# First projections of a two-layer attention backbone: products of constants ahead, a new loading order, scale and shift in one copy, context products one block late

## The chip, the cores and the metric

The kernel runs on one core of one Trainium2 chip. The metric is the device time of one execution in microseconds (us); less is better. TensorE (PE in the profile) multiplies matrices, VectorE (DVE), ScalarE (ACT) and GpSimd (POOL) work on elements, and SyncE's queue (SP) issues most DMA transfers.

## The reference, cut to what matters

Two layers over 512 latent and 256 context tokens of width 1024, all in float32. What the change touches is the head of the first layer:

```python
mod = c_silu @ ada_w + ada_b                      # for the latents; cctx_silu for the context
shift, scale, gate = jnp.split(mod, 3, axis=-1)
hx = rmsnorm(x, norm_w) * (1 + scale[:, None, :]) + shift[:, None, :]
hc = rmsnorm(cx, norm_w) * (1 + scale_c) + shift_c
px = split_cols(hx @ w_in)
pc = split_cols(hc @ w_in)
...                                               # three kinds of attention, gate, output projection
```

## The kernel before, in words

Activations lie transposed: features on the 128 partitions, tokens along the free axis. The width 1024 is 8 blocks of 128 features (`kt` 0 to 7). Set `s` = 0 is the 512 latents, `s` = 1 the 256 context tokens. Every float32 product is made from three faster ones: each operand is split into a rounded part (`hh` of the activations, `wh` of the weights) and the rest (`hl`, `wl`), and `wh*hh`, `wh*hl` and `wl*hh` are added up in PSUM.

The first stage (lines 384 to 461) makes, block by block, the normed and modulated activations, and with each block adds its part to three early projections: a query tile and a key tile of the neighbourhood attention (`WF_BQ`, `WF_BK`: 512 latent columns and 256 context columns each) and a value tile (`WT_BV`: six token tiles `t`, four of latents, two of context, 256 columns each). These sums stay open in PSUM over all eight blocks.

- `load_x(s)` (L392) loads the tokens, 8 DMAs of 256 KB for the latents and 8 of 128 KB for the context.
- `ada_load(k)` (L199) loads 1 MB of modulation weights for block k in two halves, from 9 buffers. `ada(k)` makes 8 float32 products with them (L214, 16 records in the profile), copies the result (L218), transposes it twice (L222), and gets scale and shift by small DVE operations (L225, L228, L231).
- `norm_x(s)` squares the 8 blocks on ACT (L351), adds them up on DVE (L355), sums over partitions by products with ones (L359), takes the power -0.5 (L366 on DVE, L369 on POOL), spreads the result over the partitions by transposes (L378), and copies it from PSUM to SBUF on ACT (L401).
- `make_h(kt, s)`: DVE multiplies x by scale and norm (L408), ACT adds the shift and rounds (L409, `hh`), and the rest `hl` comes from DVE in one operation (L411) where `kt % 2 == s`, and from POOL in two (L413, L414) otherwise.
- `load_w1` loads 512 columns of weights (L256, 3 buffers); `split` makes `wh` on ACT (L247) and `wl` on DVE or POOL (L250).
- `spread_silu` (L135, L138, L139) prepares rows that a much later stage uses.
- `bc`, loaded at L81, holds the q/k norm weights and the sink logits, the same on each partition; `negsink` (L89) is made from it. The first later user is L810.

The program is written with a scheduler that plays the instructions through a time model and gives each engine one fixed order; `high_priority` moves instructions ahead in it, and `after(a, b)` keeps a behind b in that order without a semaphore. The first stage ends in L430 products; then the remaining projections (L341, L318) and the attention of both layers follow.

Of the kernel before, what the change touches and what calls it, by code (L numbers as in the profile page):

```python
# [20 lines left out]
KT = 8  # L21
# [42 lines left out]
def body(tc, xT, small, bcast, rpb, adaw, adat, wt, wf, wo, trigA, trigC, mskB, mskC, outT):  # L64
# [16 lines left out]
    nc.sync.dma_start(bc, bass.AP(tensor=bcast.tensor, offset=bcast.offset, ap=[[0, 128], [1, BC_N]]))  # L81
# [7 lines left out]
    nc.vector.tensor_scalar(negsink, bc[:, BC_SINK:BC_SINK + 16], -1.0, None, op0=OP.mult)  # L89
# [105 lines left out]
    def ada_load(k, pool, tag, bufs):  # L195
        sts = []
        for half in range(2):
            st = pool.tile([128, 4, 256], F32, name="ada", tag=tag, bufs=bufs)
            nc.sync.dma_start(st, adaw[k, half])  # L199
            sts.append(st)  # L200
        return sts

    def ada(k, sts, bank):
# [5 lines left out]
        with ExitStack() as at_once:  # L209
            if k >= KT:  # L210
                at_once.enter_context(tc.high_priority(offset=2000))
            for n, half in enumerate(halves):
                for g in range(4):
                    nc.tensor.matmul(pm[32 * g:32 * g + 2, 0:256], silu_c[:, half * 4 + g, :],  # L214
                                             sts[half][:, g, :], start=(n == 0), stop=(n == 1), skip_group_check=True)
        sb = wpool.tile([128, 256], F32, name="adasb", bufs=1)
        if k < KT:
            nc.scalar.activation(sb, pm[:, 0:256], AF.Copy)  # L218
        else:
            nc.vector.tensor_copy(sb, pm[:, 0:256])  # L220
        for i in range(2):
            nc.tensor.transpose(pm[:, 256 + i * 128:384 + i * 128], sb[:, i * 128:(i + 1) * 128], ident)  # L222
        for i, (l, third, j) in enumerate(ADA[k]):
            m = modT[l, third][:, j, :]
            nc.vector.tensor_reduce(m, pm[:, 256 + i * 128:384 + i * 128].rearrange("p (g q) -> p q g", g=4)[:, 0:2, :],  # L225
                                    axis=AX.X, op=OP.add)
            if third == 1:
                nc.vector.tensor_scalar(m, m, abw[:, l, 0, j:j + 1], abw[:, l, 1, j:j + 1], op0=OP.mult, op1=OP.add)  # L228
            else:
                c = SM_AB + l * 24 + third * 8 + j  # L230
                nc.vector.tensor_scalar(m, m, sm[:, c:c + 1], None, op0=OP.add)  # L231

# [11 lines left out]
    def split(src, shape, room=None):  # L244

        hi, lo = room or [wpool.tile([128, 512], F32R, name=n) for n in ("wh", "wl")]
        nc.scalar.activation(hi, src, AF.Copy)  # L247
        wlo["n"] += 1
        eng = nc.vector if wlo["by"][wlo["n"] % len(wlo["by"])] == "D" else nc.gpsimd
        eng.tensor_sub(lo, src, hi.bitcast(F32))  # L250
# [3 lines left out]
    def load_w1(dram_ap, i, shape):  # L254
        st = wpool.tile([128, 512], F32, name="ws", bufs=CFG["ws"])
        pace["sp"] = nc.sync.dma_start(st, dram_ap[:, i * 512:(i + 1) * 512]).ins.name  # L256
        return split(st, shape)
# [126 lines left out]
    with tc.tile_pool(name="p0", bufs=1, reuse_waits="tile") as p0:  # L384
# [9 lines left out]

        def norm_x(s):
            n = SETS[s][1] - SETS[s][0]
            sums = []
            for kt in range(KT):
                add_sq(sums, xs[s, kt], kt, n, p0, lambda: Obig[:, s * 8:])
            r = p0.tile([128, n], F32, name=f"rb{s}")  # L400
            nc.scalar.activation(r, rstd_rows(sums[1], n, p0, Sbig[:, s * 512:s * 512 + n])[:, 0:n], AF.Copy)  # L401
            rb[s] = r

        def make_h(kt, s):
            A, B = [modT[0, t][:, kt, s:s + 1] for t in (1, 0)]
            n = SETS[s][1] - SETS[s][0]
            x = xs[s, kt]
            nc.vector.scalar_tensor_tensor(x, x, A, rb[s], op0=OP.mult, op1=OP.mult)  # L408
            nc.scalar.activation(hh[kt][s], x, AF.Identity, bias=B)  # L409
            if kt % 2 == s:  # L410
                nc.vector.scalar_tensor_tensor(hl[kt][s], x, B, hh[kt][s].bitcast(F32), op0=OP.add, op1=OP.subtract)  # L411
            else:
                nc.gpsimd.tensor_scalar(x, x, B, None, op0=OP.add)  # L413
                nc.gpsimd.tensor_sub(hl[kt][s], x, hh[kt][s].bitcast(F32))  # L414
# [3 lines left out]
        sts = {0: ada_load(0, p0, "ada", CFG["a0"])}  # L418
        load_x(1)
        norm_x(0)  # L420
        norm_x(1)
        early["f", WF_BQ] = [pj(), Obig[:, 0:256]]
# [4 lines left out]
        def part(key, out, a, b, kt, i):  # L427
# [5 lines left out]
            elif kt == 0:  # L433
                after(mm, opened[key].ins.name)

        for kt in range(KT):
            if kt < KT - 1:
                sts[kt + 1] = ada_load(kt + 1, p0, "ada", CFG["a0"])
            if kt % 4 == 0:
                wq = {s: load_w1(wf[0, s], kt // 4, (4, 128)) for s in (WF_BQ, WF_BK)}  # L440
            if kt % 2 == 0:
                wv = load_w1(wt[0, WT_BV, kt // 4], kt // 2 % 2, (2, 256))
            hh[kt], hl[kt] = new_h(), new_h()
            with tc.high_priority(offset=CFG["h1"]):
                ada(kt, sts.pop(kt), psT)
                for s in range(2):
                    make_h(kt, s)
                wrap_h(kt)
            for x, s in enumerate((WF_BQ, WF_BK)):
                wh, wl = wq[s]  # L450
                for g, (c0, n) in enumerate(((0, NT), (NT, NCX))):
                    for i, (a, b) in enumerate(((wh, hh), (wh, hl), (wl, hh))):
                        part(("c", 0) if g else ("l", x), early["f", s][g][:, 0:n], a[:, kt % 4, :], cols(b[kt], c0, n),
                             kt, i)
            wh, wl = wv
            for t in (1, 2, 3, 4, 5, 0):
                p = early["t", WT_BV][t // 2][:, t % 2 * 256:t % 2 * 256 + 256]
                for i, (a, b) in enumerate(((hh, wh), (hh, wl), (hl, wh))):
                    part(("v", t // 2), p, off_tile(a[kt], t), b[:, kt % 2, :], kt, i)
            if kt in (1, 2, 3, 4):  # L460
                spread_silu(kt - 1, p0)
# [1209 lines left out]
```

## Time and profile before

| | |
|---|---|
| median of 3 runs | 1198.84 us (1198.54 to 1199.2) |
| span of the profiled execution | 1197.7 us; the page lists no other time for it, and the runs stand 0.8 to 1.5 us above |
| PE busy | 1150.5 us, 96% |
| DVE / ACT / POOL busy | 769.4 / 696.9 / 408.1 us |
| granted TensorE clock, mean | 0.996 |
| first L430 product | 22.10 us after the span's start |
| last L430 product | starts at 68.80 us |

A row of the timeline gives start, duration, engine, line, operation, what is written from what, a count, and in brackets the idle time before and what ended it. A busy PE is not PE at its peak, since matmuls overlap: their pace is read from the distance of their starts. `PEld` is the loading of the stationary operand; `SPq` is an issue in SyncE's queue.

### The profile page before, as it was taken

The numbers are of one execution on the slowest core, as the hardware profiler recorded it, in microseconds if no ns is written. First come the engines' busy times: TensorE is split into PE (matmuls) and PEld (weight loads), VectorE is DVE, ScalarE is ACT, GpSimd is POOL, SyncE is SP. The second block draws the span as 40 slices with busy tenths as digits, with TensorE's granted clock in tenths as the row PEclk, the third lists the DMA queues.
The fourth block names the chain that finished last, engine by engine and source line by source line (L and its number), as shares of the span: only waits on it lengthen the run. The fifth ranks groups of instructions, "written<-read, shape, count | busy, mean of one in ns | idle before, by whom it ended". The sixth has DMA issues, their size and how long they took to land.

```text
span 1197.7 us, 21749 instructions
## 1 busy us (share of the span) xinstructions
PE 1150.5 (96%) x8016; PEld 1034.8 (86%) x8016; DVE 769.4 (64%) x1548; ACT 696.9 (58%) x1581; POOL 408.1 (34%) x496
## 2 busy tenths in 40 slices
PE   5999999999999999999999999999999999998997
PEld 3898999998898988988778999989988888887876
DVE  5767566764656665568578895567754556567563
ACT  5446555656666676588423544555666667677552
POOL 1341110234446354385000030202274563656001
PEclk9999999999999999999999999999999999999999
DMA  9552222313312112123086662323222111232152
GB/s 321 213 142 89 78 78 67 123 66 104 111 70 92 67 44 92 34 63 119 27 293 198 205 210 74 98 84 109 91 73 67 53 46 53 63 88 72 36 161 77
DMA packets 60826, 124.22 MB, mean 104 GB/s; under 512 B 7216, under 2 KB 13488, under 8 KB 60720
## 3 DMA queue, kind: packets, MB, share of 16 engines
q1 hardware_dynamic: 54768, 111.96, 29.6%
q10 hardware_dynamic: 5952, 10.88, 2.7%
q8 instruction: 63, 1.03, 0.3%
q14 instruction: 43, 0.35, 0.1%
HBM read 109.05 MB, written 11.14 MB: 100 GB/s over the span
## 4 chain that ended last, share of the span: by engine, by line
PE 81%; DVE 5%; ACT 5%; DMA 3%; issue 3%; POOL 1%; SPq 0%; ACTq 0%; DVEq 0%; POOLq 0%
PE pj L318 18%; PE pj L341 17%; PE Sbig L1049 9%; PE Obig L1049 9%; PE T L1054 9%; PE pj L519 5%; PE T L519 3%; PE Sbig L519 3%; PE T L341 2%; PE Sbig L430 2%; DVE ptl L1044 1%; DMA x<-xT_dram 1%; PE Sbig L341 1%; ACT pth L798 1%; PE pj L430 1%
## 5 line engine op out<-in xcount | busy, mean ns | idle before, releaser
L1044 DVE TENSOR_TENSOR ptl<-T,pth 128x512 fp32r<-128x512 f32 (+2 forms) x312 | 181.1, 591 | 128.6 <-ACT pth L798 126.7
L798 ACT ACTIVATE pth<-T 128x512 fp32r<-128x512 f32 (+2 forms) x312 | 158.9, 520 | 134.8 <-PE T L1054 128.1
L341 PE MATMUL pj<-wh,hL 128*128 128x256 f32 x896 | 180.6, 287 | 0.0
L318 PE MATMUL pj<-hL,wh 128*128 128x512 f32 x544 | 175.0, 401 | 0.9 <-ACT wh L247 0.5
L1054 PE MATMUL T<-ident,P 128*128 128x128 f32 x1024 | 165.7, 273 | 4.0 <-ACT qt L902 1.7
L247 ACT ACTIVATE wh<-ws 128x512 fp32r<-128x512 f32 x192 | 119.5, 629 | 78.6 <-PE pj L318 16.3
L1049 PE MATMUL Sbig<-kt,qt 128*128 128x256 f32 (+1 forms) x864 | 156.2, 308 | 4.6 <-ACT P L1160 2.5
L250 POOL TENSOR_TENSOR wl<-ws,wh 128x512 fp32r<-128x512 f32 x76 | 98.5, 1300 | 146.4 <-ACT wh L247 146.4
L341 PEld LDWEIGHTS pj<-wh,hL 128*128 128x128 f32 x896 | 144.2, 190 | 1.0 <-issue 0.2
L1049 PE MATMUL Obig<-pth,vt 128*128 128x256 f32 (+2 forms) x432 | 134.6, 321 | 4.6 <-ACT pth L798 2.0
L1054 PEld LDWEIGHTS T<-ident,P 128*128 128x128 f32 x1024 | 123.0, 140 | 17.6 <-DVE ptl L1044 2.2
L1049 PE MATMUL Obig<-ptl,vt 128*128 128x256 f32 (+2 forms) x432 | 131.4, 318 | 5.0 <-DVE ptl L1044 4.3
L1049 PEld LDWEIGHTS Sbig<-kt,qt 128*128 128x128 f32 x864 | 123.3, 189 | 13.4 <-DVE negm L1208 4.1
L341 PE MATMUL pj<-wl,hL 128*128 128x256 f32 x448 | 128.0, 286 | 0.0
L318 PEld LDWEIGHTS pj<-hL,wh 128*128 128x128 f32 x544 | 96.2, 189 | 16.7 <-ACT wh L247 0.9
L250 DVE TENSOR_TENSOR wl<-ws,wh 128x512 fp32r<-128x512 f32 x116 | 82.7, 720 | 40.4 <-ACT wh L247 31.6
L318 PE MATMUL pj<-hL,wl 128*128 128x512 f32 x272 | 107.1, 394 | 0.5 <-DVE wl L250 0.5
L1049 PEld LDWEIGHTS Obig<-pth,vt 128*128 128x128 f32 x432 | 81.6, 189 | 15.9 <-ACT pth L798 7.1
L1049 PEld LDWEIGHTS Obig<-ptl,vt 128*128 128x128 f32 x432 | 81.5, 189 | 14.7 <-DVE ptl L1044 11.3
L1445 POOL TENSOR_TENSOR bm<-wr,bm 128x192 f32<-128x192 f32 (+1 forms) x48 | 41.3, 888 | 139.6 <-DMA bm<-mskB_dram 132.4
L341 PEld LDWEIGHTS pj<-wl,hL 128*128 128x128 f32 x448 | 85.4, 191 | 0.3
L1158 DVE TENSOR_REDUCE negm<-Sbig 128x1 f32<-128x768 f32 x64 | 61.0, 953 | 29.7 <-PE Sbig L1049 15.7
(336 smaller groups left out, 2495.6 us busy)
## 6 DMA issues: line engine op xcount, KB each, us to landing
ws<-wf_dram SPq DMA_DIRECT2D x72, 256.0 KB, 3.1
ws<-wt_dram SPq DMA_DIRECT2D x72, 256.0 KB, 3.0
ada<-adaw_dram SPq DMA_DIRECT2D x32, 512.0 KB, 5.5
ws<-wo_dram SPq DMA_DIRECT2D x57, 256.0 KB, 2.8
bm<-mskB_dram SPq DMA_DIRECT2D x16, 576.0 KB, 3.7
dw<-adat_dram SPq DMA_DIRECT2D x8, 512.0 KB, 8.2
dots<-adat_dram SPq DMA_DIRECT2D x16, 256.0 KB, 4.5
u<-u ACTq DMA_DIRECT2D x9, 384.0 KB, 2.9
```

Source lines behind the costliest of these rows:

```text
L247: nc.scalar.activation(hi, src, AF.Copy)
L250: eng.tensor_sub(lo, src, hi.bitcast(F32))
L318: paced(nc.tensor.matmul(p[:, 0:n], a[:, r, :], cols(b[kt], c0, n), start=(i == 0), stop=(i == 23)), i)
L341: paced(nc.tensor.matmul(p[:, t * 256:(t + 1) * 256], tok(a[kt], t2 + t), b[:, r, :], start=(i == 0), stop=(i == 23)), i)
L430: mm = nc.tensor.matmul(out, a, b, start=begin, stop=(kt == KT - 1 and i == 2), skip_group_check=True)
L519: mm = nc.tensor.matmul(p[:, 0:n], a[:, r, :], ucols(ua[b][ft], c0, n), start=(ft == FT_ORDER[0] and i == 0), stop=(ft == FT_ORDER[-1] and ...
L798: nc.scalar.activation(out, src, AF.Copy)
L1044: i = nc.vector.tensor_sub(lo[:, 0:n], T[:, 0:n], hi[:, 0:n].bitcast(F32))
L1049: m = nc.tensor.matmul(*args, **kw)
L1054: m = nc.tensor.transpose(*args, **kw)
L1158: nc.vector.tensor_reduce(nm, S, axis=AX.X, op=OP.max, negate=True)
L1445: nc.gpsimd.tensor_add(b, src, b)
```

## The change

It does these things to the first stage, and nothing to the later ones:

1. `bc` is not loaded ahead of the tokens but at `kt == 6`, behind the last weights in SP's queue; `negsink` follows it.
2. 16 products of a constant (`identr`) with itself, 512 columns each, are issued on PE at the start (`busy`), and one product with each of the latent blocks 3 to 6 as it arrives (`busy_with`). No result of them is used.
3. The first query, key and value weights are loaded after the latents and block 0's modulation weights, ahead of the context.
4. The sum of squares leaves out the DVE addition of block 7: that block goes to the products with ones by itself.
5. `scale_x` multiplies x by the norm alone, one block ahead; block 0's reads it from PSUM, and the copy to SBUF (`keep_rb`) follows later. ACT's copy applies both scale and shift, and `hl` needs one more operation (`tensor_scalar`, then `tensor_sub`) on DVE, as it had on POOL.
6. The context products of block kt come after the latent products of block kt+1 up to kt = 3, where two blocks' worth are issued; from then on they follow their own latents. `ada(kt)`'s products stay behind the context products of block kt-2.
7. `spread_silu` moves from kt 1..4 to kt 4..7. Several ACT and DVE instructions (splits, squares of the context) get a fixed place behind others.

The core of the diff:

```diff
-    nc.sync.dma_start(bc, bass.AP(tensor=bcast.tensor, offset=bcast.offset, ap=[[0, 128], [1, BC_N]]))
-    nc.vector.tensor_scalar(negsink, bc[:, BC_SINK:BC_SINK + 16], -1.0, None, op0=OP.mult)
+    def load_bc(sp, dve):
+        i = nc.sync.dma_start(bc, bass.AP(tensor=bcast.tensor, offset=bcast.offset, ap=[[0, 128], [1, BC_N]]))
+        after(i, sp)
+        i = nc.vector.tensor_scalar(negsink, bc[:, BC_SINK:BC_SINK + 16], -1.0, None, op0=OP.mult)
+        after(i, dve)
...
+        def busy(n):
+            T = psT()
+            for _ in range(n):
+                nc.tensor.matmul(T, identr, identr[:, None, :].to_broadcast([128, 4, 128]), start=True, stop=True, ...)
+        def busy_with(x):
+            T = psT()
+            nc.tensor.matmul(T[:, 0:256], ident, x[:, 0:256], start=True, stop=True, skip_group_check=True)
...
         def norm_x(s):
-            for kt in range(KT):
-                add_sq(sums, xs[s, kt], kt, n, p0, lambda: Obig[:, s * 8:])
+            for kt in range(KT):
+                i = nc.scalar.activation(sq[:, 0:n], xs[s, kt], AF.Square)
+                if s and kt == 0:
+                    after(i, made_h["hi", 0, 0])
+                if kt in (0, KT - 1):
+                    parts.append(sq)
+                else:
+                    nc.vector.tensor_add(parts[0][:, 0:n], parts[0][:, 0:n], sq[:, 0:n])
+                if s == 0 and kt in (3, 4, 5, 6):
+                    busy_with(xs[s, kt])
+            for i, part_ in enumerate(parts):
+                ...                                  # products with ones
+            rb[s] = rstd_rows(pss, n, p0, psT() if s else Sbig[:, 0:n])[:, 0:n]
+            scale_x(0, s)
...
         def make_h(kt, s):
-            nc.vector.scalar_tensor_tensor(x, x, A, rb[s], op0=OP.mult, op1=OP.mult)
-            nc.scalar.activation(hh[kt][s], x, AF.Identity, bias=B)
-            if kt % 2 == s:
-                nc.vector.scalar_tensor_tensor(hl[kt][s], x, B, hh[kt][s].bitcast(F32), op0=OP.add, op1=OP.subtract)
-            else:
-                nc.gpsimd.tensor_scalar(x, x, B, None, op0=OP.add)
-                nc.gpsimd.tensor_sub(hl[kt][s], x, hh[kt][s].bitcast(F32))
+            i = nc.scalar.activation(hh[kt][s], x, AF.Identity, bias=B, scale=A)
+            e = nc.vector if kt % 2 == s else nc.gpsimd
+            e.tensor_scalar(x, x, A, B, op0=OP.mult, op1=OP.add)
+            i = e.tensor_sub(hl[kt][s], x, hh[kt][s].bitcast(F32))
...
         load_x(0)
         sts = {0: ada_load(0, p0, "ada", CFG["a0"])}
+        for ap in (wf[0, WF_BQ], wf[0, WF_BK], wt[0, WT_BV, 0]):
+            ...                                      # the three first weights
         load_x(1)
+        busy(16)
+        norm_x(0); ada(0); make_h(0, 0); first splits; keep_rb(0)      # in this order
         norm_x(1)
+        keep_rb(1)
...
         for kt in range(KT):
+            ...                                      # weights of blocks 2, 4, 6; ada_load(kt + 1) behind them
+                if kt:
+                    ada(kt, sts.pop(kt), psT, ended.get(kt - 2))
+                    make_h(kt, 0)
+            products(kt, 0, wq, wv)                  # latents
+            held.append((kt, 1, wq, wv))
+                make_h(kt, 1)
+            if kt:
+                products(*held.pop(0))               # context
+            if kt == 3:
+                products(*held.pop(0))
+            if kt < KT - 1:
+                for s in range(2):
+                    scale_x(kt + 1, s)
+            if kt == 6:
+                load_bc(pace["sp"], made_h["lo", 6, 0])
+            if kt >= 4:
+                spread_silu(kt - 4, p0)
```

More of the change, by code (lines that the diff above doesn't have):

```diff
@@ L193, in step, with ada_load @@
                 self.load()
[L195 removed]
+    def ada_load(k, pool, tag, bufs, behind=None):
         sts = []
@@ L434, in part @@
                 after(mm, opened[key].ins.name)
-        for kt in range(KT):
[L437 to L448, printed above, removed]
+            return mm
```

100 lines of the change are left out of this document (76 added, 24 removed).

## The prediction, made before the change was run

> **What bounds the kernel now.** I read the page first: span and busy shares.
>
> ```profile
> span 1197.7 us, 21749 instructions
> PE 1150.5 (96%) x8016; PEld 1034.8 (86%) x8016; DVE 769.4 (64%) x1548; ACT 696.9 (58%) x1581; POOL 408.1 (34%) x496
> ```
>
> PE is the bound, so only PE's quiet time can be won. Next, the view by stages: stretch, its length, busy us and count of PE, PEld, DVE, ACT and POOL, granted clock, DMA share, GB/s.
>
> ```profile
> 0.00:22.10 22.10, 8.43 (x54) 4.98 (x55) 11.77 (x37) 12.36 (x24) 1.75 (x8) 1.00 0.87 288
> 22.10:32.33 10.23, 9.66 (x70) 5.70 (x71) 7.44 (x19) 5.38 (x14) 5.06 (x5) 1.00 1.03 407
> 32.33:68.92 36.59, 36.59 (x301) 32.12 (x302) 23.01 (x51) 17.95 (x44) 15.43 (x14) 1.00 0.54 181
> ```
>
> From 32.33 PE is full to the end of the stage; nothing can be won there. What can be won lies before 32.33. How much, I get from the pace of matmuls in the full stretch (timeline of PE, start to start).
>
> ```profile
> 34.20 0.28 PE L430 MATMUL Sbig<-wh,hL 128*128 128x256 f32 x1
> 34.32 0.28 PE L430 MATMUL Sbig<-wl,hL 128*128 128x256 f32 x1
> 66.20 0.40 PE L430 MATMUL pj<-hL,wl 128*128 128x512 f32 x1
> 66.43 0.39 PE L430 MATMUL pj<-hL,wh 128*128 128x512 f32 x1
> 45.25 1.91 PE L214 MATMUL T<-ada,silu_c 128*2 128x256 f32 x32
> 47.09 0.39 PE L430 MATMUL Sbig<-wh,hL 128*128 128x256 f32 x1
> 41.18 0.38 PE L222 MATMUL T<-ident,adasb 128*128 128x128 f32 x2
> ```
>
> 256 columns take 0.12 us, 512 take 0.23. A block's latents are 6 products of 512 and 12 of 256 columns, 2.82 us; its context 12 of 256, 1.44. `ada` of two blocks (32 records) takes 47.09 - 45.25 = 1.84, so 0.92 each; with two transposes (I take 0.2) 1.12. A `spread_silu`, four transposes, is 0.4 at the same pace. The stage's work is 8 x (2.82 + 1.44 + 1.12) + 4 x 0.4 = 44.6 us. The full stretch did 36.59, of which 7 products (0.84) were borrowed from the next stage. So by 32.33 PE had done 44.6 - 36.59 + 0.84 = 8.9 us and had lost 23.4. That sum is what the change can shrink; the forecast compares it with the time lost before PE is full in the changed kernel.
>
> **The change, part by part.**
>
> *`bc` last.*
>
> ```profile
> 1.17 0.42 SPq L81 DMA_DIRECT2D bc<-bcast_dram  x1
> 2.50:3.00 0.50, 0.00 (x0) 0.00 (x0) 0.47 (x5) 0.22 (x1) 0.00 (x0) 1.00 0.75 74
> 5.50:6.00 0.50, 0.00 (x0) 0.00 (x0) 0.04 (x1) 0.00 (x0) 0.00 (x0) 1.00 1.06 396
> 5.96 0.17 DVE L89 TENSOR_SCALAR negsink<-bc 128x16 f32<-128x16 f32 x1 [2.77 <-DMA bc<-bcast_dram]
> 6.73 2.75 ACT L351 ACTIVATE sq<-x 128x512 f32<-128x512 f32 x4 [4.00 <-DMA x<-xT_dram]
> ```
>
> Until `bc` has landed the DMA engines are three quarters busy but move only 74 GB/s; then 396. So 136 KB cost some 2 us of the loading. Bounds: 0.5 (only its issue, 0.42) and 2.4 (everything before 5.5 moved at 396). I take 1.9: the engines were busy with something, and only `bc` was there besides the tokens. Behind the last weights its DMA has cover, and on DVE `negsink` has the last block's operations queued behind it, and PE waits for those; I estimate the issue near 33, when block 3's modulation buffers are free, and DVE's turn near 46. Without that cover it costs up to 5.96 - 1.17 = 4.8 us.
>
> *The way to the first product.*
>
> ```profile
> 8.12 5.47 DVE L355 TENSOR_TENSOR sq<-sq 128x512 f32<-128x512 f32 x7 [1.99 <-ACT sq L351]
> 13.83 1.87 PE L359 MATMUL Obig<-ones,sq 128*128 128x2 f32 x8
> 15.98 1.03 POOL L369 TENSOR_TENSOR rstd<-rstd,mhalf 128x4 f32<-128x4 f32 x1 [14.70 <-DVE rstd L366]
> 19.56 1.03 PE L214 MATMUL T<-ada,silu_c 128*2 128x256 f32 x8
> 21.28 0.61 PE L214 MATMUL T<-ada,silu_c 128*2 128x256 f32 x8
> 19.63 0.74 DVE L408 SCALAR_TENSOR_TENSOR x<-x,mod,rb 128x512 f32<-128x512 f32 x1
> 20.41 0.72 ACT L409 ACTIVATE hL<-x,mod 128x512 fp32r<-128x512 f32 x1
> 22.10 0.74 PE L430 MATMUL pj<-hL,wh 128*128 128x512 f32 x2 [0.21 <-ACT wh L247]
> ```
>
> Now the additions begin at 8.12, 0.78 each. The changed kernel begins them at 8.12 - 1.9 = 6.2 and makes six: 10.9. Then two sets of products with ones (16 records instead of 8). The products of constants matter here: the same 8 `ada` records take 1.03 at 19.56 and 0.61 at 21.28, so PE runs slow until about 21, although the clock column shows 1.00 there; after them it should be fast. At the slow 0.23 per record 16 take 3.7; at half, 1.85, which I take: 12.9. Power and its neighbours 1.35 (14.25), four transposes 0.6 (L222's two are 0.38 at the fast pace; 14.85), scaling 0.75 (15.6; the read from PSUM priced by the same row, and the copy of the norm leaves the path; the first value products still wait for that copy, since the norm lies in their bank, but PE has block 0's query and key products before them), ACT's copy 0.75: first product at 16.4, 5.7 earlier. The first weights now come before the context, 0.75 MB sooner, so the wait for them that ends just before 22.10 goes. The products of constants themselves: 20 of them, at most 20 x 0.43 = 8.6 (twice the fast 0.23, rounded down) from 1.7, so over by 10.3, before the ones at 10.9; hidden by 0.6, and what they overrun is paid in full.
>
> *Block 1's modulation is late next.* Its two halves now:
>
> ```profile
> 14.42 0.89 SPq L199 DMA_DIRECT2D ada<-adaw_dram  x2
> DMA to landing us min/median/max: 3.8/4.6/5.4
> 37.80 0.39 ACT L218 ACTIVATE adasb<-T 128x256 f32<-128x256 f32 x1 [1.16 <-PE T L214]
> 49.28 0.24 DVE L225 TENSOR_REDUCE mod<-T 128x2 f32<-128x8 f32 x2 [0.69 <-PE T L222]
> 49.49 0.29 DVE L228 TENSOR_SCALAR mod<-mod,abw 128x2 f32<-128x2 f32 x1
> 49.68 0.23 DVE L231 TENSOR_SCALAR mod<-mod,sm 128x2 f32<-128x2 f32 x1
> 51.67 1.57 POOL L413 TENSOR_SCALAR x<-x,mod 128x512 f32<-128x512 f32 x1 [5.39 <-ACT hL L409]
> 53.32 1.28 POOL L414 TENSOR_TENSOR hL<-x,hL 128x512 fp32r<-128x512 f32 x1
> 56.53 1.08 POOL L413 TENSOR_SCALAR x<-x,mod 128x256 f32<-128x256 f32 x1 [1.93 <-ACT hC L409]
> 57.70 0.74 POOL L414 TENSOR_TENSOR hC<-x,hC 128x256 fp32r<-128x256 f32 x1
> ```
>
> They land at 18.7 to 19.8. In the changed kernel 0.75 MB of weights go ahead of them, 1.9 us at 396 GB/s, and `bc`'s 1.9 are gone: about 19.3 again. From there: half of `ada` 0.46, copy 0.39, transposes 0.38, 0.24, 0.29, 0.23, four hand-overs of 0.05, ACT's copy 0.72: block 1's `hh` at 22.2. Block 0's latents, 2.82 us from 16.4 and slowed by the splits on ACT and DVE, are done by about 19.5, so PE waits. Block 1's `hl` is POOL's: 1.57 + 1.28, 25.1; then POOL makes block 0's context rest, 1.08 + 0.74, 26.9 (I take the context's norm as ready by then; what it is later than about 24 adds directly). With the last third of those products PE is there at 27.4. `ada(2)`, pinned behind them, takes 0.92, and 2.5 by the rows above to `hh`: 30.8. Meanwhile PE has block 1's context and `ada(3)`, 1.44 + 1.12 + 1.12 from 27.4: 31.1, and is full from there; from kt = 4 on `ada` is a block ahead. The work done by 31.1 is two blocks of latents and context, 8.52, and four `ada`, 4.48: 13.0. Lost: 18.1. Gain 23.4 - 18.1 = 5.3.
>
> *Cooling.* PE's quiet time between 19.5 and 22.2, with only `ada(1)` in it, resembles this stretch before a wait for weights:
>
> ```profile
> 620.00:624.00 4.00, 2.35 (x10) 1.29 (x8) 3.96 (x7) 1.46 (x3) 0.00 (x0) 1.00 1.02 377
> 624.00:628.00 4.00, 2.88 (x7) 2.31 (x8) 4.00 (x8) 0.79 (x2) 0.00 (x0) 0.65 1.02 374
> ```
>
> There the granted clock falls to 0.65. If it falls at 22.2, the next products run at half pace for about as long, and the 27.4 becomes 28.5: bounds 0 and 1.1; I take 0.6, since the alignment is open. The Trainium skill, "TensorE: Matmul & The Clock Gate", Part 1, says that the clock halves after an idle window of about 3.4 us whose phase runs free; by that rule the stretch from 12.9 to 16.4, too, would cool, the constants would be half in vain, and with 22.2 cool as well the sum would be 4.2 instead of 5.3: block 0's latents at half pace, 5.6 us, still end by 22.0.
>
> *The rest.* DVE's extra operation in `hl` (8 more): between 0.23 (L231, two columns) and 0.74 (L408, 512) each; beside PE's full stretch, where DVE is busy 23 of 36.59 us, it costs nothing. POOL's count is unchanged. `spread_silu` moves inside the full stretch, the same PE time. SP's queue issues the same DMAs; the weights of blocks 2, 4, 6 stand ahead of `ada_load`, whose data are then 5 us or more ahead. Later stages I take to shift as a whole. Sum: 5.3 - 0.6 = 4.7 against 1197.7, so a span of 1193.0; the runs' median stands 1.1 above the span: 1194.1.
>
> **The rivals.**
>
> *Full sooner (gain 6.3 to 8.1).* If block 1's modulation lands 2 us sooner or the context fills the wait, PE is full from about 22.2 with 2.82 + 2.24 done: lost 17.1, gain 6.3; in the best case it is full from 16.4 with 1.12 done: lost 15.3, gain 8.1. For it: nothing but modulation is missing then. Against it: POOL's 2.85 for `hl`. Time 1190.7 to 1192.5.
>
> *DVE and POOL in each other's way (gain 2).*
>
> ```profile
> 53.32 1.31 DVE L231 TENSOR_SCALAR mod<-mod,sm 128x2 f32<-128x2 f32 x1
> ```
>
> A scalar operation on DVE that starts with POOL's subtraction at 53.32 lasts as long as that, 1.31 instead of 0.23. The change adds eight such operations. Two of them on the path, block 0's and block 2's, cost 2 x 1.3: gain 2.1, 1196.7. Against it: POOL is idle at block 0, and most lie in the full stretch. The Trainium skill, "SBUF — State Buffer", "Who interferes with whom", calls this an exclusive lock that `tensor_scalar` can take; the rows agree.
>
> *Given back later (no change).* If the first attention starts at the time it does now, the gain becomes a wait. The row of the bias tables, and that of the stretch in which PE is first not full again:
>
> ```profile
> 79.32 2.19 POOL L1445 TENSOR_TENSOR bm<-wr,bm 128x192 f32<-128x192 f32 x3 [3.44 <-issue]
> 92.80:99.30 6.50, 5.97 (x42) 5.08 (x42) 5.25 (x11) 4.88 (x12) 0.00 (x0) 1.00 0.28 86
> ```
>
> The tables are done at 81.5, 11 us before that, so even in their old place they would not hold the attention back for a gain of 4.7: against it. For it: DVE and ACT, not PE, pace that stretch. Time 1198.5.
>
> *Slower: the pin on `ada`.* `ada(kt)` stands behind the context products of kt-2. Where nothing else is ready, each block pays 0.92 + 2.5 less 1.44 of context, 2.0 us. With n blocks beyond the second it loses 18.7 + 2.0 n; from n = 3 it loses more than 23.4. With five (blocks 3 to 7): 28.7, 5.3 slower, 1204.1. Against it: from kt = 4 on the pin lies a block back. It needs a scheduler that doesn't use that.
>
> **How the numbers follow.** Forecast 1194.1, chance 0.54, its own range 1192.5 to 1196.3 (cooling 0 to 1.1, `bc` 0.5 to 2.4, landing of block 1 one us either way); full sooner 0.18; lock 0.09; given back 0.08; pin 0.11. 0.2% is 2.4 us, about what a measurement here can tell from no change. Faster: the first two and the edge of the lock, 0.73; same: the lock and the give-back, 0.15; slower: the pin and a rest, 0.12. The range leaves out the pin and the far end of the best case: 1190.2 to 1198.8.
>
> **What would show it.** Right: tokens' squares from about 4.8, the first L430 product near 16.4, a wait of some 3 us before block 1's `hh` at 22, PE full from about 31, the last L430 product near 64. Wrong: squares still from 6.7; `ada` records at 1.03 after the constants; quiet PE beyond 35; the first stage's end 5 us earlier but the attention's start not.

## The result: 27 us slower, and the profile after

The changed kernel takes 1226.01 us (1223.31 to 1227.24), the kernel before 1199.02 (1198.54 to 1199.83): ratio 1.0216, 95% interval 1.02 to 1.0232 (the two medians divide to 1.0225, inside that interval). The forecast was 1194.1. First the span and the busy shares, from the page of the changed kernel.

```profile
span 1225.4 us, 21842 instructions
PE 1172.8 (96%) x8052; PEld 1050.5 (86%) x8052; DVE 773.6 (63%) x1554; ACT 697.4 (57%) x1581; POOL 406.4 (33%) x496
```

PE is busy for 22 us more. The 20 products without use are some 9 of these (5.7 for the sixteen, 2.0 and 1.2 for the four). The rest is 12 more records with ones and, for the most part, the same work at a slower clock. The way to the first product (timelines of ACT, DVE and PE of the changed kernel):

```profile
4.04 0.63 ACT L423 ACTIVATE sq<-x 128x512 f32<-128x512 f32 x1 [1.31 <-DMA x<-xT_dram]
5.48 0.69 DVE L429 TENSOR_TENSOR sq<-sq 128x512 f32<-128x512 f32 x1 [2.29 <-ACT sq L423]
7.38 3.88 DVE L429 TENSOR_TENSOR sq<-sq 128x512 f32<-128x512 f32 x5 [1.20 <-ACT sq L423]
11.31 2.78 PE L435 MATMUL Obig<-ones,sq 128*128 128x2 f32 x16 [1.80 <-DVE sq L429]
15.08 1.89 PE L220 MATMUL T<-ada,silu_c 128*2 128x256 f32 x16
16.90 1.12 PE L389 MATMUL Sbig<-ident,rstd 128*128 128x128 f32 x4
20.17 1.31 PE L496 MATMUL pj<-hL,wh 128*128 128x512 f32 x2 [1.73 <-ACT hL L460]
```

The squares begin 2.7 us sooner than before (4.04, not 6.73), though the sums then wait for later tokens and end at 11.26. But the first product comes at 20.17, only 1.9 sooner, since everything on PE between is at half pace: 16 `ada` records take 1.89, where they take 1.05 at 51.98. The view by stages says why (length, busy us and count of PE, PEld, DVE, ACT, POOL, granted clock, DMA share, GB/s):

```profile
8.00:12.00 4.00, 2.20 (x11) 1.29 (x11) 3.11 (x6) 2.61 (x5) 0.00 (x0) 1.00 1.02 400
12.00:16.00 4.00, 4.00 (x26) 2.79 (x29) 0.16 (x1) 0.00 (x0) 1.03 (x1) 0.53 1.06 358
16.00:20.00 4.00, 2.44 (x18) 1.18 (x10) 1.81 (x6) 1.60 (x3) 0.00 (x0) 0.50 0.92 316
20.00:24.00 4.00, 3.62 (x8) 2.46 (x9) 3.85 (x7) 2.85 (x9) 0.00 (x0) 0.50 0.90 335
```

From 8 to 12 PE waits for the sums of squares and is busy 2.20 of 4 us; at 12 the clock falls to 0.53 and stays at half until 24. Then block 1's modulation and the pinned ones (SP's issue of block 1's and 2's weights, then PE):

```profile
15.07 1.85 SPq L203 DMA_DIRECT2D ada<-adaw_dram  x4
26.81 1.05 PE L435 MATMUL Obig<-ones,sq 128*128 128x2 f32 x8 [0.57 <-DVE sq L429]
29.26 1.89 PE L220 MATMUL T<-ada,silu_c 128*2 128x256 f32 x16
43.14 1.04 PE L220 MATMUL T<-ada,silu_c 128*2 128x256 f32 x16
46.76 1.22 PE L496 MATMUL pj<-hL,wh 128*128 128x512 f32 x2 [1.63 <-ACT hL L460]
51.98 1.05 PE L220 MATMUL T<-ada,silu_c 128*2 128x256 f32 x16
55.65 0.74 PE L496 MATMUL pj<-hL,wh 128*128 128x512 f32 x2 [0.51 <-ACT hL L460]
58.16 0.39 PE L496 MATMUL Obig<-hC,wh 128*128 128x256 f32 x1 [1.41 <-DVE hC L464]
61.78 1.05 PE L220 MATMUL T<-ada,silu_c 128*2 128x256 f32 x16
68.79 0.50 PE L496 MATMUL pj<-hL,wh 128*128 128x512 f32 x1 [0.47 <-DVE hL L464]
```

`ada(1)` starts at 29.26, 14 us after its DMA was issued, behind the context's norm (26.81). Its data are not what it waits for: they landed at most 5.9 us after their issue, by 21.4. `ada(2)`, (3) and (4) start at 43.14, 51.98 and 61.78. Behind the first two PE waits for `hh` (1.63 and 0.51 before the row, as much as 0.5 more at the transposes), and at 58.16 for DVE's `hl` of the context. PE is full from 68.79, not from 31.

The last product of the stage starts at 91.0, 22.2 us later than before. The third softmax row of the first attention starts at 122.43 against 96.31, 26.1 later; the spans differ by 27.7. So in these two traces some 22 us are lost in the first stage, 4 between it and the attention, under 2 behind.

The stage in stretches of 12 us, of before, of the changed kernel, and of two experiments that are told below (e10 without the pin, e16 the same with the pin):

```profile
24.00:36.00 12.00, 11.43 (x91) 7.64 (x90) 8.92 (x23) 6.08 (x15) 6.06 (x6) 1.00 1.03 399
36.00:48.00 12.00, 12.00 (x115) 9.53 (x114) 6.37 (x15) 6.34 (x16) 4.67 (x4) 1.00 0.72 268
48.00:60.00 12.00, 12.00 (x98) 10.67 (x97) 9.31 (x23) 5.06 (x13) 4.67 (x4) 1.00 0.19 67
```

```profile
24.00:36.00 12.00, 8.77 (x51) 5.83 (x49) 5.85 (x18) 5.32 (x12) 3.60 (x5) 0.78 0.54 213
36.00:48.00 12.00, 9.10 (x47) 7.43 (x48) 4.11 (x12) 2.09 (x5) 1.13 (x2) 0.65 0.55 197
48.00:60.00 12.00, 9.59 (x66) 7.54 (x66) 5.85 (x13) 4.50 (x10) 3.97 (x4) 0.93 0.07 24
60.00:72.00 12.00, 10.74 (x94) 8.11 (x93) 6.83 (x20) 5.92 (x13) 3.17 (x3) 1.00 0.61 208
```

```profile
24.00:36.00 12.00, 11.50 (x105) 8.98 (x94) 9.32 (x29) 7.97 (x20) 6.73 (x7) 1.00 0.66 248
36.00:48.00 12.00, 12.00 (x108) 10.15 (x107) 7.86 (x16) 5.47 (x13) 4.50 (x5) 1.00 0.96 350
48.00:60.00 12.00, 12.00 (x107) 9.49 (x99) 6.98 (x19) 5.25 (x13) 2.43 (x4) 1.00 0.26 89
```

```profile
24.00:36.00 12.00, 10.23 (x58) 8.23 (x51) 5.97 (x17) 5.40 (x13) 4.10 (x5) 0.71 0.79 303
36.00:48.00 12.00, 10.28 (x89) 7.55 (x88) 4.09 (x13) 2.96 (x7) 2.63 (x2) 1.00 0.45 172
48.00:60.00 12.00, 10.01 (x74) 7.26 (x73) 4.86 (x9) 4.24 (x9) 2.04 (x2) 0.86 0.56 185
60.00:72.00 12.00, 10.23 (x77) 8.47 (x78) 9.15 (x23) 5.12 (x12) 4.48 (x4) 1.00 0.13 46
```

In the changed kernel PE is quiet for 9.8 of these 48 us (four times 12 less the busy time), and what it does until 60 is done at 0.65 to 0.93 of the clock, worth about 5.8 more (busy time by what the clock lacks: 1.9 + 3.2 + 0.7). That is some 15 of the 22 us; part of the rest lies before 24, where the clock is at half from 12 on. So most of these waits cost twice: the quiet, and the slow clock behind it. Not all do: the waits at 55.65 and 58.16 are followed by a clock of 1.00.

### The profile page after: what moved, and what is told of

Its sections match the earlier page's. It is cut to its first block, busy times and chain, and to the rows that moved or that the text cites. A ratio compares the mean times of both kernels' runs of the same rounds, so it can differ in the third digit from the quotient of the medians.

```text
span 1225.4 us, 21842 instructions
## 1 busy us (share of the span) xinstructions
PE 1172.8 (96%) x8052; PEld 1050.5 (86%) x8052; DVE 773.6 (63%) x1554; ACT 697.4 (57%) x1581; POOL 406.4 (33%) x496
## 4 chain that ended last, share of the span: by engine, by line
PE 79%; DVE 7%; ACT 5%; DMA 4%; issue 3%; POOL 1%; SPq 0%; ACTq 0%; DVEq 0%; POOLq 0%
PE pj L329 18%; PE pj L352 17%; PE Sbig L1136 9%; PE Obig L1136 9%; PE T L1141 9%; PE pj L606 4%; PE T L606 3%; PE Sbig L606 2%; PE Sbig L496 1%; ACT pth L885 1%; DVE ptl L1131 1%; PE Sbig L352 1%; DVE junk L157 1%; DMA xr<-xT_dram 1%; PE pj L496 1%
## 5 line engine op out<-in xcount | busy, mean ns | idle before, releaser
L1136 PEld LDWEIGHTS Obig<-ptl,vt 128*128 128x128 f32 x432 | 81.9, 190 | 14.1 <-DVE ptl L1131 10.9
```

The costliest lines, as they stand in the source:

```text
L1136: m = nc.tensor.matmul(*args, **kw)
```

## The experiments

Ratios are to the kernel before, with 95% intervals; "changed" is the changed kernel. "Last product" is the start of the stage's last product in the profile. A profile is of one run (of the changed kernel it is the slowest of four, of e2 and e10 the fastest), so this column tells where time goes, and the ratio how much.

| run | edit | ratio | last product |
|---|---|---|---|
| changed | | 1.0216 (1.02 to 1.0232) | 91.0 |
| e1 | changed, no pin on `ada` | 1.0137 (1.0117 to 1.0156) | 78.1 |
| e2 | changed, bank of its own | 1.0188 (1.0156 to 1.0219) | 84.4 |
| e3 | e1 + e2 | 1.0099 (1.0082 to 1.0115) | 76.0 |
| e4 | changed, no constants | 1.0213 (1.019 to 1.0237) | 92.0 |
| e5 | before, `bc` last | 1.0004 (0.9993 to 1.0014) | 68.9 |
| e6 | e5 + first weights ahead | 1.0068 (1.0055 to 1.008) | 73.9 |
| e7 | e3 + bias strip behind weights | 1.0060 (1.0039 to 1.0082) | 76.7 |
| e8 | e3 + more constants | 1.0075 (1.006 to 1.009) | 81.2 |
| e9 | e7, splits and loads not pinned | 1.0077 (1.0055 to 1.0099) | 74.7 |
| e10 | e7 + early spreads | 1.0015 (1.0002 to 1.0027) | 70.8 |
| e11 | e9 + early spreads, context not late | 1.0025 (1.0012 to 1.0038) | 71.7 |
| e12 | before, new scale and shift | 1.0031 (1.0019 to 1.0042) | 72.3 |
| e13 | before, late spreads | 1.0003 (0.9991 to 1.0015) | 71.1 |
| e14 | e10, old scale and shift | 1.0014 (1.0002 to 1.0025) | 72.1 |
| e15 | e3 + early spreads | 1.0017 (1.0003 to 1.003) | 72.5 |
| e16 | e10 + the pin again | 1.0144 (1.0119 to 1.0169) | 85.2 |
| e17 | changed, no pin, early spreads | 1.0068 (1.005 to 1.0087) | 74.2 |
| e18 | e16, pin three blocks back | 1.0046 (1.0032 to 1.0061) | 70.3 |

**The pin (e1, e3, e16, e18).**

```diff
-                    ada(kt, sts.pop(kt), psT, ended.get(kt - 2))
+                    ada(kt, sts.pop(kt), psT)                      # e1; e18: ended.get(kt - 3)
```

> The changed kernel without the rule that ada(kt)'s products stay behind the context products of block kt-2. Theory 'pin': in the changed kernel PE waits three times for a modulation that was pinned too late (44.2 to 46.8, 53.6 to 58.2, 64.7 to 68.8 us in its trace), some 9 us; without the pin these waits go and the time falls from 1226 to about 1217. Theory 'bank' (block 1's modulation stands behind the context's norm, because that norm's transposes take one of the two T banks ahead of it): this alone costs nearly all, and the time stays above 1222; block 1's ada products still start near 29.

> The kernel of the run with the spreads at their old place (ratio 1.0015), with the pin of the modulation products behind the context's products of two blocks before put back; all else stays mended. Theory 'the pin costs by itself': each modulation of blocks 2 to 7 begins only when the context of two blocks before is done, and what it feeds is 2.5 to 3.5 us later; 8 to 10 us as in the two pairs of runs with and without it: ratio 1.008 to 1.010, 1211 to 1213 us. Rival 'it cost only together with the late spreads and the bank': 1.0015 to 1.004.

> The kernel of the run with the pin put back (1216.4 us, ratio 1.0144), with one number changed: the modulation of a block stands behind the context's products of three blocks before instead of two. In the run with the pin at two, PE has 7 to 21 products in each 4 us from 36 to 64 where the run without a pin has 14 to 29. Theory 'the pin costs the chain from the modulation to hi, 3.8 us, less what PE has to do meanwhile': a block of latents and context, 4.26 us, now lies between, so it is hidden: 1.001 to 1.004. Rival 'any order held by hand costs, since the loads and buffers follow it': 1.008 to 1.012.

Without the pin 1.0137 instead of 1.0216, 0.8%; on top of the bank 0.9% (e3 against e2); with everything else mended 1.3%, 15.5 us of 1200 (e16 against e10), more than expected. The two last fences above are this pair: with the pin PE is quiet for 1.7 to 2.0 us in each 12 us until 72, without it after 36 not at all. It is the largest of the causes measured here. One block further back it costs 0.3% instead of 1.3 (e18), just above what the theory there allowed, and the stage ends as soon as without it (70.3 against 70.8); where the 0.3% arise was not shown.

**The bank (e2, e3, e17).** The norm of the context takes one of the two rotating PSUM banks, ahead of `ada(1)` in the program, and `ada(1)` then waits for the context's squares and sums. That the banks are handed out in the program's order is my reading of it; what the edit shows is that `ada(1)` no longer waits once the norm has a bank of its own.

```diff
-            rb[s] = rstd_rows(pss, n, p0, psT() if s else Sbig[:, 0:n])[:, 0:n]
+            rb[s] = rstd_rows(pss, n, p0, Sbig[:, 1024 * s:1024 * s + n])[:, 0:n]
```

> The changed kernel with one edit: the context's norm is spread over the partitions in the third value bank (Sbig), which is not used before the context's products, and not in a T bank. Theory 'bank': ada(1)'s products run near 21 instead of 29.3, and the time falls by about 8 us to 1218, and by more if PE's clock cools less. Theory 'pin': the first products come earlier, but the pinned ada(2) still ends the stage; less than 3 us are won.

> Both edits. If the two losses add up, 1226 - 9 - 8 = about 1209. If the cool clock and the later waits for weights and bias tables follow from the same late stage, all of the 27 us come back and more: 1195 to 1200, with PE full from about 32. If a third cause holds the stage (weights pinned behind the context's activations in SP's queue), it stays above 1212.

> The changed kernel with two of its parts undone and nothing else: no pin on the modulation products, the spreads behind blocks 1 to 4. Its order of instructions has both halves of the rotary tables ahead of the first bias table, but the context's norm still takes a PSUM bank ahead of block 1's modulation. Theory 'these two parts are the loss, and the bank costs only a little': 1.0015 to 1.004, 1202.5 to 1206 us. Rival 'the bank costs 0.4% by itself, as in the two pairs of runs with and without it': 1.005 to 1.007, 1207 to 1209.

PE of e2, `ada(1)` and `ada(2)`:

```profile
21.19 1.88 PE L220 MATMUL T<-ada,silu_c 128*2 128x256 f32 x16
34.59 1.05 PE L220 MATMUL T<-ada,silu_c 128*2 128x256 f32 x16
```

`ada(1)` starts 8.1 us sooner than in the changed kernel, near 21 as the theory "bank" said, but the pinned `ada(2)` still comes 13.4 us behind it. So little of the 8 us reaches the end: alone 0.3%, with overlapping intervals; with the pin gone 0.4% (e3 against e1), and 0.5% with early spreads (e17 against e15), both clear of each other. PE in e17, then in e15, which has the bank:

```profile
24.77 1.05 PE L435 MATMUL Obig<-ones,sq 128*128 128x2 f32 x8 [0.75 <-DVE sq L429]
26.85 0.52 PE L389 MATMUL T<-ident,rstd 128*128 128x128 f32 x2 [1.03 <-POOL rstd L380]
27.30 1.89 PE L220 MATMUL T<-ada,silu_c 128*2 128x256 f32 x16
```

```profile
23.70 2.69 PE L220 MATMUL T<-ada,silu_c 128*2 128x256 f32 x24
27.23 1.05 PE L435 MATMUL Obig<-ones,sq 128*128 128x2 f32 x8
```

With its own bank the norm comes behind the modulation, which starts 3.6 us sooner.

**The constants (e4, e8).** e4 leaves `busy` and `busy_with` out; e8 adds four products of constants behind each `busy_with`.

> The changed kernel without the 16 + 4 products of constants and tokens on PE. Theory 'in vain': PE is quiet from 8 to 11 us and cools before the real products, so the time stays within 2 us of 1226; and since the last of these products stands behind the products with ones and ahead of ada(0), the first L496 product comes up to 1 us earlier than 20.2. Theory 'they warm': the products with ones and ada(0) take longer, and the time rises by 2 us or more.

> The changed kernel without the pin of the modulation products and with the context's norm in a PSUM bank of its own (1211.55 us as measured), with four more products of constants of 512 columns behind each of the four products with the tokens, so that PE is kept busy from 4 to 12 us (they leave no result behind). Theory 'clock': in the trace without this edit PE is busy 2.17 of the 4 us from 8 to 12 and the granted clock is 0.5 from 12 to 24 us and 0.77 until 28; PE is busy 9.7 us of 12 to 24 at half pace, so some 5 us are lost. With the clock at 1.00 from 12 on, 16 records of the first modulation take about 1 us instead of 1.9 and the stage ends 4 to 5 us sooner: 1206 to 1208 us, ratio 1.005 to 1.007. Rival 'the loads bound it': the products become fast and wait for the modulation weights instead: 1210 to 1212. Rival 'it cools later': the clock is at 1.00 at 12 but falls in the quiet of 16 to 20 us; a gain of 1 to 2 us only.

e4: no difference (1.0213 against 1.0216); its first product is at 20.40, 0.2 us later. So the constants are in vain, as the first theory of e4 said. e8 against e3: 0.24% less, the intervals overlap, and its last product is even 5 us later. In its view by stages the clock holds to 20 us and then falls, the third case of the expectation:

```profile
16.00:20.00 4.00, 1.73 (x22) 0.77 (x14) 2.47 (x8) 2.17 (x5) 0.73 (x1) 1.00 0.98 336
20.00:24.00 4.00, 2.24 (x14) 0.72 (x18) 3.53 (x7) 2.66 (x9) 0.00 (x0) 0.61 0.98 347
24.00:28.00 4.00, 4.00 (x22) 1.46 (x14) 0.00 (x0) 0.00 (x0) 0.00 (x0) 0.53 1.02 412
```

**The loads (e5, e6).** e5 moves only `bc` on the kernel before; e6 also loads the first three weights ahead of the context.

> The kernel before, with one part of the change alone: the broadcast of the norm weights is issued behind the last weights of the first stage; all else is as before. Theory 'right term': in the trace after the change the squares begin at 4.04 us instead of 6.73, so the broadcast costs 2.7 us of the first loading. The first product stood behind the tokens' norm (22.10 us), so about 2 of these 2.7 us should reach the end, the rest going to the first weights, which land only just in time (a wait of 0.21 us stands before the first product): 1198 to 1198.8 against 1200.3 for the kernel before, ratio 0.9980 to 0.9987. Rival 'the weights take its place': the first product goes from 22.1 to about 20.5 only and PE is filled by nothing else until the stage's loads are in; within 0.1% of before. Rival 'no gain at all, the term was wrong': squares at 4 us but the first product still at 22.

> The kernel before, with two parts of the change: the norm weights' broadcast behind the last weights, and the first three weight loads ahead of the context's tokens. Theory 'loading bounds the start': the first weights then land 1.9 us sooner and the wait that ends at the first product goes, so the first product comes at about 19.3 and the whole is 2.7 us faster than before: 1197 to 1198, ratio 0.9972 to 0.9985. Rival 'the context becomes late': the context's norm and block 1's modulation land 1.9 us later, which eats what the weights gain: as the run with the broadcast alone, or slower than it by up to 1.9 us (ratio 0.9985 to 1.001).

Both gains that I expected were missing. In e5 the first product comes at 21.05 instead of 22.10, and from 24 to 36 us PE runs 104 records where it ran 91 (records of unlike size):

```profile
24.00:36.00 12.00, 12.00 (x104) 9.26 (x103) 6.41 (x21) 5.54 (x14) 6.51 (x6) 1.00 1.03 401
```

The last product starts at 68.86, before at 68.80: the lead is gone by the end of the stage. From 36 to 48 us PE runs 103 records where it ran 115, busy all the time in both; where the lead went was not settled. In e6 the weights cost 0.6%: PE is quiet for 0.4, 0.5 and 1.0 us in the three stretches of 4 us from 52 on. That the context and its norm become late was the rival; that it is the reason here was not shown.

**The queue (e7, e15, e9).** SP issues in order. In e3, SP's third bias strip (`wr`, one buffer) waits for POOL's second bias table, and the first attention's weights stand behind it; then ACT and PE wait:

```profile
86.06 7.44 SPq L1524 DMA_DIRECT2D wr<-rpb_dram  x2
93.60 6.31 SPq L267 DMA_DIRECT2D ws<-wt_dram  x4
98.20 0.63 ACT L255 ACTIVATE wh<-ws 128x512 fp32r<-128x512 f32 x1 [7.09 <-DMA ws<-wt_dram]
100.41 0.47 PE L329 MATMUL pj<-hC,wh 128*128 128x256 f32 x2 [3.30 <-DVE gt L967]
```

```diff
+            if l == 0 and h == 2:
+                after(i, pace["sp"])          # e7: this strip's DMA behind the weight loads
```

> The changed kernel without the pin of the modulation products and with the context's norm in a PSUM bank of its own (1211.55 us as measured), and one DMA moved: the third strip of the relative bias is issued behind the four weight loads that stood behind it on SP's queue. In the trace without this edit that DMA waited from 86.06 to 93.5 us for the second bias table of POOL, the four weight loads were issued from 93.60, ACT waited 7.09 us for them, and PE stood still for 3.3 us at 97 us and then ran at a granted clock of 0.62 from 100 to 104. Theory 'queue order': the weights are issued at about 90.3, when their buffers come free, and land by 93; the quiet stretch and the slow one after it go, 3.3 and about 1.5 us: 1206 to 1208 us, ratio 1.005 to 1.007. Rival 'other work is late as well' (DVE's splits, the softmax): the quiet moves by a few us and the time stays within 1210 to 1212.

> The kernel of the run with the bias strip moved behind the weights (1208.9 us, ratio 1.0060), with one more part of the change undone: the splits of the weights of blocks 2, 4 and 6 no longer stand behind the block before (hi and lo of its context), and the modulation loads no longer behind the weight loads. In the trace without this edit SP's queue stands from 23.6 to 36.22 us before a weight load whose buffer the pinned split holds, the DMA engines are busy 0.53 and 0.01 of 28 to 36 us, and four modulation loads stand behind it. Theory 'queue held by the pin': the loads run through to about 44 as in the kernel before, and the quiet of 1.44 us of PE at 52 to 60 goes: 1206 to 1207.5 us, ratio 1.0035 to 1.005. Rival 'the late loads were not the bound': PE has enough to do from 32 to 52 either way, and the quiet at 52 to 60 comes from the chain of the modulation and the late spreads: 1208 to 1210.

> The kernel of the run with the spreads at their old place (ratio 1.0015), without the edit that moved the third bias strip behind the weights on SP's queue. With early spreads POOL's instructions have both halves of the rotary tables ahead of the first bias table, as in the kernel before. Theory 'the late spread pushed the bias table back': the edit is no longer needed, and the time stays at 1.0005 to 1.0025. Rival 'the queue needs its own mending': 4 to 5 us slower, ratio 1.0045 to 1.006.

e7 against e3: 0.4% less (1.0060 against 1.0099; the intervals touch), as the queue's theory said, and its trace has no such wait: from 88 to 104 us only 0.38 us stand before a product. The changed kernel has the wait too (`wr` 7.15 us at 101.57, PE 3.49 us before 115.60), which fits the 4 us lost between its stage and the attention. e9 undoes the fixed places of splits and modulation loads: no gain, so its rival stands. e15: with early spreads the edit is worth nothing (1.0017 against 1.0015).

**The spreads (e10, e13).**

```diff
-            if kt >= 4:
-                spread_silu(kt - 4, p0)
+            if kt in (1, 2, 3, 4):
+                spread_silu(kt - 1, p0)
```

> The kernel of the run with the bias strip moved behind the weights (1208.9 us, ratio 1.0060), with one more part of the change undone: the four spreads of the conditioning stand behind blocks 1 to 4 again, not 4 to 7. In the trace without this edit the spreads are at 51.21, 54.97, 56.26 and 64.75 us among the modulations of the last blocks; each takes a PSUM bank of the same two, a copy of 0.60 us on ACT and a DMA on SP, and PE is quiet for 1.44 us at 52 to 60 (one wait there is for the copy of a spread). Theory 'the spreads stand in the modulation's way': block 6's modulation comes sooner, products between 52 and 60 rise from 24 towards 45 as in the kernel before, the stage ends 2 to 3 us sooner: 1205.5 to 1207 us, ratio 1.003 to 1.0045. Rival 'moved to the cold start': at blocks 1 to 4 they cost what they save: 1208 to 1210.

> The kernel before with one part of the change alone: the four spreads of the conditioning stand behind blocks 4 to 7 instead of 1 to 4. In its order of instructions POOL makes the first bias table between the two halves of the rotary tables, as in the changed kernel. Theory 'the late spread alone carries the two last terms': the spreads stand among the last modulations (quiet at 52 to 60, some 2 to 5 us) and the weights of the first attention wait behind the third bias strip on SP's queue (some 4.7 us): 1205 to 1211, ratio 1.004 to 1.0085. Rival 'only together with the new order': before has slack at both places, and the time stays within 0.15% of before.

Early spreads are worth 0.45% on e7 and 0.8% on e3 (e15). Part of it lies in the stage: from 48 to 60 us PE is busy 10.56 us in e7 and 12.00 in e10. With them the scheduler gives POOL both halves of the rotary tables ahead of the first bias table, as before; with late ones the bias table comes between. On the kernel before the same late spreads cost nothing that could be measured (e13), although POOL's order and the queue's wait appear there as well. SP, then PE of e13:

```profile
80.31 7.21 SPq L1437 DMA_DIRECT2D wr<-rpb_dram  x2
87.61 6.26 SPq L256 DMA_DIRECT2D ws<-wt_dram  x4
94.36 0.47 PE L318 MATMUL pj<-hC,wh 128*128 128x256 f32 x2 [2.05 <-DVE gt L880]
```

PE waits there for 2.05 us, not 3.30, with the clock at 1.00. 2 us are 0.17%, and e13's interval reaches to 0.15%: whether something pays for them or they are in part lost in the noise was not settled.

**Scale, shift and the rest of the order (e12, e14, e11).** e12 makes only `hh` and `hl` in the new way on the kernel before; e14 takes the old way in e10; e11 undoes every other part of the order.

> The kernel before with one part of the change alone: x is multiplied by the norm on DVE, ACT's copy scales and shifts, and the rest is made by a scale-and-shift and a subtraction on DVE or POOL (eight more operations on DVE, the same count on POOL); the order of the blocks, the loads and the rest are as before. Theory of the prediction 'hidden': within 0.1% of before. Rival 'lock': DVE's subtraction lasts as long as POOL's that it meets, 1.45 instead of 0.45 us, some 1 to 3 times on the path: 1 to 3 us slower, ratio 1.001 to 1.0025. Rival 'shorter path': ACT's copy needs no scaled x, only the norm, so each block's hi is ready 0.3 us after the modulation instead of 1.1: up to 2 us faster, ratio 0.998 to 0.9995.

> The kernel of the run with the spreads at their old place (ratio 1.0015: changed kernel without the pin, bank of its own, bias strip behind the weights, early spreads), with the old scale and shift: norm and scale in one DVE operation, ACT adds only the shift, the rest in one DVE operation or two on POOL. Theory 'the new scale and shift are the rest': alone on the kernel before they cost 0.31%, so without them 0.9985: about 1199 where the kernel before has 1200.75, faster than both. Rival 'they cost nothing in this order' (the x products are made ahead, a block early): 1.0005 to 1.002.

> The kernel of the run with the bias strip moved behind the weights (1208.9 us, ratio 1.0060), with all the rest of the new order undone: the pins of the splits and modulation loads, the late spreads, and the context a block behind. What is left of the change is the constants, the norm weights last, the first weights ahead of the context, the new scale and shift, and the order up to block 0's products. Theory 'the new order is the loss': the first stage ends near 69 to 71 as in the kernel before, 1201 to 1204 us, ratio 0.9995 to 1.0025. Rival 'weights ahead of the context': as in the run where these were moved alone on the kernel before (ratio 1.0068), the context's norm and block 1's modulation are late and the time stays at 1206 to 1210. Rival 'the new scale and shift': the lock of DVE by POOL (1.46 us instead of 0.45) keeps it at 1205 to 1208.

Alone the new way costs 0.3%, in e10 nothing (e14). e11, at 1.0025, is not told apart from e10: the context a block behind and the fixed places of splits and loads, taken together, neither gain nor cost in that order. DVE and POOL of e12 show the lock:

```profile
39.19 1.48 DVE L411 TENSOR_TENSOR hC<-x,hC 128x256 fp32r<-128x256 f32 x1
26.65 0.69 DVE L411 TENSOR_TENSOR hL<-x,hL 128x512 fp32r<-128x512 f32 x1
39.09 1.29 POOL L411 TENSOR_TENSOR hL<-x,hL 128x512 fp32r<-128x512 f32 x1
```

256 columns take 1.48 us beside POOL's subtraction, 512 take 0.69 alone. That the lock makes up the whole 0.3% was not shown.

No version beats the kernel before: e5, e10, e13, e14 and e15 lie within 0.2% of it.

## Why the prediction was wrong, step by step

- *`bc`*: right and under-sized. 2.7 us of loading, where I took 1.9 between bounds of 0.5 and 2.4. The sums end at 11.26 all the same, where I had 10.9, since later tokens hold them up. And its worth at the end is nothing that could be measured (e5).
- *The way to the first product*: forecast 16.4, came at 20.17. The mis-sized terms: 16 records with ones 2.78 instead of 1.85, `ada` 1.89 where I took it as hidden, four transposes 1.12 instead of 0.6. I took for granted that constants leave the clock at full pace, and priced cooling only from 22.2 on (0.6). The constants were over by 7.3, PE was busy 2.2 of the next 4 us, and the clock was at half from 12 to 24. The Trainium skill, "TensorE: Matmul & The Clock Gate", Part 1, ties the fall to an idle window of about 3.4 us; here it came with no quiet longer than 1.80 us. The Trainium skill, same page, section "A second HAM failure mode: psum-queue depth-cycling", tells of a kernel in which frequent short gaps between groups of products made the clock swing. That is nearer, but not the same: here gaps of 0.24 and 1.80 us came before the fall. I had the first rule in a side sentence, with a sum of 4.2 instead of 5.3; that, too, was far too small.
- *Block 1's modulation is late next*: right that it is, wrong on what it waits for. I followed its data (landing at 19.3). It stood behind the context's norm for a PSUM bank, and started at 29.26 (21.19 with a bank of the norm's own). Nothing in the working asked in which order the two banks are handed out. Worth 0.3 to 0.5%.
- *"Meanwhile PE has block 1's context and `ada(3)`"*: this is the step that failed most. `ada(3)` is pinned behind block 1's context, and that stands behind block 2's latents, which need `ada(2)`: so nothing is left to fill the wait. The rival "the pin on `ada`" had the mechanism and a chance of 0.11; its price was 2.0 us a block over five blocks, 10 us, where the three pairs of runs give 9.5, 10.7 and 15.5. The waits lie at fewer blocks than five, but the clock falls behind them (0.65 on the mean of 36 to 48, and 0.71 and 0.86 in e16 where e10 has 1.00). The argument against it, that the pin lies a block further back from `kt` = 4 on, held (`ada(4)` and `ada(5)` follow each other, and PE is full from 68.79), but the time was gone by then.
- *`spread_silu` "the same PE time"*: wrong. I counted its PE time and not what its place does to the order of other engines: 0.45 to 0.8% in this order, nothing measurable in the old one.
- *DVE's extra operations "cost nothing"*: wrong alone (0.3%), right in the mended order. The rival "lock" had the right mechanism, though in e12 it is the subtraction that lasts as long as POOL's (1.48 us); the scalar operations take 0.41 to 0.97.
- *"Later stages shift as a whole"*: wrong by 4 of the 27 us, where the rows show the wait in SP's queue (7.15 us).

The terms do not add up from single edits on the kernel before: weights ahead of the context cost 0.6% there, and e10 holds them at a total of 0.15%. What is shown is the way from 1.0216 to 1.0017 by three edits (pin, bank, spreads: 0.8 + 0.4 + 0.8%), and that nothing is gained by what is left.

## What to carry to other kernels

Before you price an order held by hand, write down for each held instruction what it waits for and what would run in the meantime, and follow that two blocks on: if the filler is held as well, the wait is paid each time, and a slow clock behind it. Count a moved step's buffers (PSUM banks, single-buffer tiles, the place in SP's queue) and what the scheduler does with the rest, not only its own time. An earlier start is worth nothing unless the end of its stage moves too.

## What the runs showed of the hardware

- The clock fell with PE busy for 2.20 of 4 us and no quiet over 1.80 us (changed kernel, 8 to 12), and was not back before 24 us. In this trace the clock changes up to 53 us come at multiples of 3.41 us from each other; the four falls follow stretches of that length with PE busy 1.61 to 1.82 us, and it held after 2.40 and 2.01 us (53.17 to 60.00). A limit can't be read from it: in e10 the clock fell after 2.59 busy us (10.27 to 13.68).
- The clock column reads 1.00 also where PE runs at half pace at its first start: without constants (e4) 16 `ada` records take 1.89 us in a stretch marked 1.00:

```profile
15.31 1.89 PE L220 MATMUL T<-ada,silu_c 128*2 128x256 f32 x16
16.00:20.00 4.00, 2.67 (x18) 1.29 (x10) 1.72 (x6) 1.37 (x3) 0.70 (x1) 1.00 0.93 326
```

  The pace of the records is the sounder measure. The trace holds the clock as a list of changes, whose first entry is at 27.0 us in e4, 5.4 in the changed kernel and 21.0 in the kernel before; the 1.00 ahead of it is no measurement.
- A broadcast of 136 KB to 128 partitions held up the loading by 2.6 us (e5, where it is the only edit: the squares begin at 4.09 instead of 6.73); its issue alone takes 0.42.
